# Stores of ScalarE's results: from SyncE's queue to ScalarE's own

## The chip, the cores and the metric

The kernel runs on one core of one Trainium2 chip. The core has five engines, each with its own stream of instructions that it works through in order: TensorE (PE: matmuls, and PEld, the loads of its weights), VectorE (DVE), ScalarE (ACT), GpSimd (POOL) and SyncE (SP), which here only issues transfers (DMAs). They wait for each other through semaphores. Transfers between the chip's main memory and the core's own memory are issued by an engine and carried out by 16 DMA engines. The metric is the device time of one execution in microseconds (us).

## The reference, cut to what matters

Two blocks over a sequence of 2048 positions of width 1024, in float32. The first normalizes, projects, and runs a diagonal state-space scan (S5) over one half of the channels beside a gated short convolution over the other; the second is a modulated layer with a convolution, a bidirectional state-space scan (SSD), a Fourier mix and a gated feed-forward net.

```python
def first_block(x, norm_gain, w_in, ssm_..., w_glu, b_glu, conv_w, w_out, final_norm_gain):
    xn = rmsnorm(h, norm_gain)
    proj = xn @ w_in                       # u_ssm, z_ssm, h_conv, b_conv, c_conv, z_conv
    y_ssm = s5_mixer(u_ssm, ...) * silu(z_ssm)      # scan, gelu, then a gate by w_glu
    y_conv = short_conv_mixer(h_conv, b_conv, c_conv, conv_w) * silu(z_conv)
    h = h + concat(y_ssm, y_conv) @ w_out
    return rmsnorm(h, final_norm_gain)

def second_block(x, c, ctx, c_ctx, w_ada, ...):
    mx = silu(c) @ w_ada + b_ada           # shifts, scales and gates (modulation)
    hx = modulate(rms_norm(x, g_pre_mix), sm_x, cm_x)
    u_f, z, xs, B, C, dt = mixer_inputs(hx, w_in, conv_w, ...)
    y = ssd_bidir(xs, B, C, dt, ...)
    x = x + gm_x * rms_norm(mixer_output(u_f, z, xs, y, ...), g_post_mix)
    x = x + gf_x * rms_norm(swiglu(modulate(...), w_gate, w_up, w_down), g_post_ffn)
```

## The kernel before

The sequence is cut into four blocks of 512 positions (b = 0 to 3). All products are made by `mtile`: a weight tile of 128 x 1024 is loaded (`wraw`, three buffers, L110), ACT casts it to its upper part (`whi`, two buffers, L112), DVE or POOL makes the rest (`wlo`, L115), and PE runs 24 matmuls of 512 columns: 16 with `whi` (L126, L127) and 8 with `wlo` (L130). So for each weight tile PE needs one cast of ACT.

Stages, as they lie in the profile's time: parameters of the scan and the first projection of blocks 0 and 1 (`a1_units`, `s5_params`; 0 to 350 us); the projection of blocks 2 and 3, woven with the scan (`s5_units`), the modulation (`mod_units`) and the first block's gate and output (`a2_units`; 350 to 830 us); the rest of these with the context (830 to 1090 us); stage B, the second block's projection and convolution (`b_units`; 1090 to 1650 us); then scan, mix and feed-forward net.

`s5_units` runs two halves of the sequence (tb) with eight channel groups (cg) each. `enter` loads Ug, s5G (one buffer) and a table, makes two banks of products (L660, L662: eight matmuls each), and DVE scans them (L666 to L683); `leave` loads s5C (one buffer) and s5M, makes the output with 12 matmuls (L704 to L706), and ACT puts it through a gelu into Yg (L707). After every second group Yg, which has 128 partitions, is stored to Yd in main memory by 16 transfers of 16 x 8 x 64 elements (L712). There are eight such bursts in the program, 128 transfers. `mod_units` is a chain of 48 steps: each multiplies the two halves of a weight tile that the step before it has loaded (L940, `mraw`, two buffers in all) and then issues the two loads for the next (L951).

The other stores of the change: Ud, Gd and ZSd before 830 us, and in stage B UFd, XTd, XSd, BTd, CTd, SBd and a part of Z2d, each one transfer behind the ACT instruction that makes its result.

The program is written in Python against a tile framework: a scheduler with priorities (`high_priority` raises those of the weights' loads and casts) puts the instructions of each engine in order, and hands each transfer one of eight completion counters in turn, whichever engine issues it. A transfer waits until the one before it on its counter, that is the transfer eight earlier, has landed. In the kernel before, SP issues all 2037 transfers in one queue.

Of the kernel before, what the change touches and what calls it, by code (L numbers as in the profile page):

```python
# [17 lines left out]
P = 128  # L18
# [43 lines left out]
class Kernel:  # L62
# [335 lines left out]
    def s5_params(self, pp):  # L398
# [124 lines left out]
        def matrices(bt):  # L523
# [56 lines left out]
            nc.scalar.mul(Gt[:, :, P + 64:256], pv[:, :, 0], -1.0)  # L580
            nc.sync.dma_start(out=self.Gd[bt], in_=Gt)
            pk = self.bank("ss")
# [53 lines left out]
    def s5_units(self, tb, sp):  # L636
# [49 lines left out]
        def leave(cg):  # L686
# [21 lines left out]
            if q == 1:  # L708
                c0 = qt * 128
                for t in range(T8):  # L710
                    for i in range(2):
                        nc.sync.dma_start(  # L712
                            out=self.Yd[2 * tb + i, c0:c0 + 128, t, :].rearrange("(g h) k -> h g k", h=GH),
                            in_=Yg[t * GH:(t + 1) * GH, :, i * 64:(i + 1) * 64])
# [62 lines left out]
    def a1_units(self, b, ops):  # L777
# [13 lines left out]
        def u(j):  # L791
# [6 lines left out]
            else:  # L798
                nc.scalar.copy(uk, kt(ps))
            nc.sync.dma_start(out=self.Ud[tb, j * P:(j + 1) * P, :, hf * 64:(hf + 1) * 64],  # L800
                              in_=us.rearrange("p (t k) -> p t k", t=T8))
# [40 lines left out]
        def zs(j):  # L842
            ps = mt(4 + j)
            t = self.tmp("zs")
            silu(t, ps)
            nc.sync.dma_start(out=self.ZSd[b, :, j], in_=t)

# [293 lines left out]
    def uf_dt(self, x, c, X, b):  # L1141
# [11 lines left out]
        if b is not None:  # L1153
            u = self.tmp("uf", (P, FW))
            nc.scalar.copy(u, ps[:, 0:FW])
            nc.sync.dma_start(out=self.UFd[4 * b + c], in_=u)

# [68 lines left out]
    def b_units(self, b, ops, bp):  # L1226
# [22 lines left out]
        def conv(m):  # L1249
# [7 lines left out]
            def turn():  # L1257
                if m < 6:
                    self.transposes(s, TB, st["xs"][:, :, m * P:(m + 1) * P])
                    if m == 5:  # L1260
                        nc.sync.dma_start(out=self.XTd[b], in_=st["xs"])
                elif m < 10:
# [4 lines left out]
            if m < 6:  # L1267
                nc.sync.dma_start(out=self.XSd[b, :, m], in_=s)
            elif m < 10:
                nc.sync.dma_start(out=self.BTd[b, :, m - 6], in_=s)  # L1270
            else:
                nc.sync.dma_start(out=self.CTd[b, :, m - 10], in_=s)

        def gate(m):
# [7 lines left out]
            else:  # L1282
                nc.scalar.activation(z, ps, AF.Silu)
            nc.sync.dma_start(out=self.Z2d[b, :, m], in_=z)

# [3 lines left out]
        def state(c):  # L1289
# [7 lines left out]
            for g, ps in self.states(st["xw"], st["B"], c):  # L1297
# [3 lines left out]
                nc.scalar.copy(sb[:, hs], ps[:, 192:384].rearrange("p (r e) -> p r e", r=HG))  # L1301
            nc.sync.dma_start(out=self.SBd[4 * b + c].rearrange("p (h e) -> p h e", e=64), in_=sb)
            if c < 3:
# [654 lines left out]
```

## Time and profile before

| | |
|---|---|
| median of 3 runs | 3636.63 us (3629.4 to 3638.18) |
| profiled execution | 3634.7 us, of which the span of the core is 3632.8 us |
| PE busy | 3462.0 us (95%) |
| DVE, ACT, POOL busy | 2147.9, 1461.9, 965.3 us |
| granted clock of PE, mean | 0.98 |

The span is the time from the first to the last instruction. Busy is the time in which an engine has an instruction at work; waiting, and issuing a transfer, are not counted. The granted clock is that of PE, as a share of full speed. The views behind the prediction are shown as rows further down.

### The profile page before, as it was taken

The page shows a single profiled execution, that of the slowest core. Times are in us where ns is not written, and L with a number is a line of the kernel's source. Part 1 is how long each engine was busy: PE and PEld are TensorE (multiplying, and loading weights), DVE is VectorE, ACT ScalarE, POOL GpSimd, SP SyncE. Part 2 cuts the span into 40 slices and gives each one's busy share as a digit, 9 for nine tenths or more (in the row PEclk, how much of TensorE's full clock was granted, in tenths as well). Part 3 has the DMA queues.
Part 4 walks back from the last instruction along what each step waited for, and adds up shares of the span by engine and source line. Part 5 has one row for each costly group of instructions (what it writes and reads, how often), then busy time and mean ns, then how long its engine had stood idle before and what let it go on. Part 6 is the DMA issues. An engine that isn't in the chain of part 4 may idle for free.

```text
span 3632.8 us, 46986 instructions
## 1 busy us (share of the span) xinstructions
PE 3462.0 (95%) x16602; PEld 2831.0 (78%) x16602; DVE 2147.9 (59%) x3991; ACT 1461.9 (40%) x2350; POOL 965.3 (27%) x931
## 2 busy tenths in 40 slices
PE   8899999988989999999999999999999999999998
PEld 6677888776778888876777788877888778887887
DVE  8765534446687577777756544566445664454334
ACT  3233232234444344335535533355333553343222
POOL 1764233232353453343213101131011220110001
PEclk9999999999989999999999999999999999999999
DMA  6467565677654565466554334443345443444232
GB/s 199 156 190 223 191 210 175 203 230 241 211 191 153 178 204 172 163 205 203 164 186 137 118 111 155 155 149 120 111 135 171 140 130 111 127 153 130 83 113 76
DMA packets 322508, 588.14 MB, mean 162 GB/s; under 512 B 73952, under 2 KB 150624, under 8 KB 321376
## 3 DMA queue, kind: packets, MB, share of 16 engines
q1 hardware_dynamic: 322272, 585.13, 51.1%
q8 instruction: 132, 2.16, 0.2%
q14 instruction: 104, 0.85, 0.1%
HBM read 472.63 MB, written 112.36 MB: 161 GB/s over the span
## 4 chain that ended last, share of the span: by engine, by line
PE 60%; DVE 6%; DMA 4%; ACT 2%; issue 1%; POOL 1%; SPq 0%; POOLq 0%; DVEq 0%; ACTq 0%
PE mm L130 17%; PE mm L126 17%; PE mm L127 17%; PE ss L1125 1%; PE nb L940 1%; PE ss L1473 1%; PE ss L1523 1%; DVE cy L1038 1%; DMA outT<-n_t 1%; PE nb L1501 1%; PE ss L1138 1%; PE mm L1149 1%; PE mm L1150 0%; PE mm L1151 0%; PE nb L192 0%
## 5 line engine op out<-in xcount | busy, mean ns | idle before, releaser
L112 ACT CAST whi<-wraw 128x1024 fp32r<-128x1024 f32 (+3 forms) x634 | 568.9, 898 | 1044.3 <-PE mm L127 758.0
L115 DVE TENSOR_TENSOR wlo<-wraw,whi 128x1024 fp32r<-128x1024 f32 (+3 forms) x516 | 538.2, 1044 | 698.2 <-PE mm L130 487.3
L126 PE MATMUL mm<-xh,whi 128*128 128x512 f32 (+1 forms) x2000 | 801.2, 403 | 49.4 <-ACT whi L112 30.1
L127 PE MATMUL mm<-xl,whi 128*128 128x512 f32 (+1 forms) x2000 | 787.8, 396 | 5.8 <-DVE xl L142 3.6
L152 POOL TENSOR_TENSOR n_acc<-n_acc,n_sq 128x512 f32<-128x512 f32 (+1 forms) x175 | 229.5, 1315 | 1365.5 <-ACT n_sq L151 1337.9
L126 PE MATMUL mm<-dxh,whi 128*128 128x512 f32 x1408 | 549.9, 391 | 1.7 <-ACT dxh L997 1.7
L127 PE MATMUL mm<-dxl,whi 128*128 128x512 f32 x1408 | 548.6, 390 | 1.6 <-DVE dxl L998 1.5
L130 PE MATMUL mm<-xh,wlo 128*128 128x512 f32 (+1 forms) x2000 | 500.2, 392 | 9.9 <-DVE wlo L115 9.6
L126 PEld LDWEIGHTS mm<-xh,whi 128*128 128x128 f32 x2000 | 385.7, 193 | 138.7 <-ACT whi L112 40.9
L127 PEld LDWEIGHTS mm<-xl,whi 128*128 128x128 f32 x2000 | 385.7, 193 | 86.1 <-DVE xl L142 6.6
L130 PEld LDWEIGHTS mm<-xh,wlo 128*128 128x128 f32 x2000 | 375.7, 191 | 89.9 <-DVE wlo L115 12.9
L115 POOL TENSOR_TENSOR wlo<-wraw,whi 128x1024 fp32r<-128x1024 f32 (+1 forms) x118 | 284.1, 2410 | 549.0 <-ACT whi L112 268.0
L130 PE MATMUL mm<-dxh,wlo 128*128 128x512 f32 x1408 | 349.7, 389 | 0.0
L126 PEld LDWEIGHTS mm<-dxh,whi 128*128 128x128 f32 x1408 | 264.1, 188 | 57.7 <-ACT dxh L997 3.0
L127 PEld LDWEIGHTS mm<-dxl,whi 128*128 128x128 f32 x1408 | 264.3, 188 | 57.2 <-DVE dxl L998 2.8
L130 PEld LDWEIGHTS mm<-dxh,wlo 128*128 128x128 f32 x1408 | 263.6, 188 | 54.3
L126 PE MATMUL mm<-hh,whi 128*128 128x512 f32 (+1 forms) x744 | 285.5, 390 | 5.0 <-ACT hh L141 4.7
L1038 DVE SCALAR_TENSOR_TENSOR cy<-mm,vecs,cy 128x504 f32<-128x504 f32 (+5 forms) x396 | 266.9, 690 | 27.6 <-ACT cy L1032 24.4
L127 PE MATMUL mm<-hl,whi 128*128 128x512 f32 (+1 forms) x744 | 280.5, 382 | 2.0 <-DVE hl L142 2.0
L130 PE MATMUL mm<-hh,wlo 128*128 128x512 f32 (+1 forms) x744 | 199.3, 383 | 0.0
L126 PEld LDWEIGHTS mm<-hh,whi 128*128 128x128 f32 x744 | 139.7, 189 | 36.7 <-ACT hh L141 9.4
L127 PEld LDWEIGHTS mm<-hl,whi 128*128 128x128 f32 x744 | 140.5, 189 | 30.4 <-DVE hl L142 5.2
(473 smaller groups left out, 4510.7 us busy)
## 6 DMA issues: line engine op xcount, KB each, us to landing
wraw<-w_in SPq DMA_DIRECT2D x186, 512.0 KB, 4.5
wraw<-w_gate SPq DMA_DIRECT2D x88, 512.0 KB, 3.7
wraw<-w_up SPq DMA_DIRECT2D x88, 512.0 KB, 3.6
wraw<-w_out SPq DMA_DIRECT2D x64, 512.0 KB, 3.9
mraw<-w_ada SPq DMA_DIRECT2D x96, 256.0 KB, 3.7
n_x<-xT SPq DMA_DIRECT2D x85, 256.0 KB, 4.7
n_x<-X1d SPq DMA_DIRECT2D x80, 256.0 KB, 4.0
n_x<-X2d SPq DMA_DIRECT2D x72, 256.0 KB, 4.0
```

Source lines behind the costliest of these rows:

```text
L112: nc.scalar.copy(hi, raw)
L115: eng.tensor_tensor(lo, raw, hi.bitcast(F32), ALU.subtract)
L126: nc.tensor.matmul(ps, lhsT=hi[:, s], rhs=xh, start=k == ks[0], stop=False)
L127: nc.tensor.matmul(ps, lhsT=hi[:, s], rhs=xl, start=False, stop=False)
L130: nc.tensor.matmul(ps, lhsT=lo[:, s], rhs=rhs(k)[0], start=False, stop=k == ks[-1])
L152: nc.gpsimd.tensor_tensor(acc, acc, sq, ALU.add)
L940: nc.tensor.matmul(ps, lhsT=raws[k // 4][:, k % 4 * P:(k % 4 + 1) * P], rhs=sc[:, k, 0:n], start=k == 0, stop=k == KD - 1)
L1038: nc.vector.scalar_tensor_tensor(yr[:, :, lo:hi], pr[:, :, lo + d:hi + d], w(k), yr[:, :, lo:hi], ALU.mult, ALU.add)
L1125: nc.tensor.matmul(ps, lhsT=B_tm[:, c, g], rhs=xw[:, g].rearrange("p d r e -> p (d r e)"), start=True, stop=True)
L1138: nc.tensor.transpose(ps[:, c], src[:, c * P:(c + 1) * P], self.ident)
L1149: nc.tensor.matmul(ps, lhsT=ah, rhs=wh[:, s], start=(k == 0), stop=False)
L1473: nc.tensor.matmul(ps, lhsT=CT[:, g, c * P:(c + 1) * P], rhs=hFB[:, g].rearrange("p d e -> p (d e)"), start=True, stop=True)
```

## The change

At ten places `nc.sync.dma_start` becomes `nc.scalar.dma_start`: the stores of results that ACT makes are issued by ACT itself, all other transfers by SP as before. Where ACT makes the result in some blocks only (Ud for b > 0, Z2d for b = 0), so does the choice of queue. It is 262 transfers of 2037: Yd 128, Ud 12, ZSd 16, Gd 8, UFd 16, XTd 4, XSd 24, BTd 16, CTd 16, Z2d 6, SBd 16.

```diff
@@ matrices of the scan
-            nc.sync.dma_start(out=self.Gd[bt], in_=Gt)
+            nc.scalar.dma_start(out=self.Gd[bt], in_=Gt)
@@ s5_units, leave
-                        nc.sync.dma_start(
+                        nc.scalar.dma_start(
                             out=self.Yd[2 * tb + i, c0:c0 + 128, t, :].rearrange("(g h) k -> h g k", h=GH),
                             in_=Yg[t * GH:(t + 1) * GH, :, i * 64:(i + 1) * 64])
@@ a1_units, u and zs
-            nc.sync.dma_start(out=self.Ud[tb, j * P:(j + 1) * P, :, hf * 64:(hf + 1) * 64],
+            (nc.scalar if b else nc.sync).dma_start(out=self.Ud[tb, j * P:(j + 1) * P, :, hf * 64:(hf + 1) * 64],
                               in_=us.rearrange("p (t k) -> p t k", t=T8))
-            nc.sync.dma_start(out=self.ZSd[b, :, j], in_=t)
+            nc.scalar.dma_start(out=self.ZSd[b, :, j], in_=t)
@@ stage B
-            nc.sync.dma_start(out=self.UFd[4 * b + c], in_=u)
+            nc.scalar.dma_start(out=self.UFd[4 * b + c], in_=u)
-                        nc.sync.dma_start(out=self.XTd[b], in_=st["xs"])
+                        nc.scalar.dma_start(out=self.XTd[b], in_=st["xs"])
-                nc.sync.dma_start(out=self.XSd[b, :, m], in_=s)
+                nc.scalar.dma_start(out=self.XSd[b, :, m], in_=s)
-                nc.sync.dma_start(out=self.BTd[b, :, m - 6], in_=s)
+                nc.scalar.dma_start(out=self.BTd[b, :, m - 6], in_=s)
-                nc.sync.dma_start(out=self.CTd[b, :, m - 10], in_=s)
+                nc.scalar.dma_start(out=self.CTd[b, :, m - 10], in_=s)
-            nc.sync.dma_start(out=self.Z2d[b, :, m], in_=z)
+            (nc.sync if b else nc.scalar).dma_start(out=self.Z2d[b, :, m], in_=z)
-            nc.sync.dma_start(out=self.SBd[4 * b + c].rearrange("p (h e) -> p h e", e=64), in_=sb)
+            nc.scalar.dma_start(out=self.SBd[4 * b + c].rearrange("p (h e) -> p h e", e=64), in_=sb)
```

The scheduler orders the program anew with it: all engines' orders differ in the first 1700 us or so, and ACT has four more loads of its function tables.

First place, the fourth burst of Yd (Yg_4382). ACT before: the casts whi follow Yg directly.

```order
L707 ACT_TABLE_LOAD
L707 ACTIVATE Yg_4382<-ss_4775 128x512
L141 CAST xh_4130<-n_t_4805 128x512
L112 CAST whi_4881<-wraw_4879 128x1024
L799 COPY us_4842<-mm_4817 128x64x8
L112 CAST whi_4915<-wraw_4913 128x1024
L799 COPY us_4876<-mm_4851 128x64x8
L112 CAST whi_4949<-wraw_4947 128x1024
```

ACT now:

```order
L707 ACT_TABLE_LOAD
L707 ACTIVATE Yg_4382<-ss_4775 128x512
L712 DMA Yd<-Yg_4382 16x8x64
L112 CAST whi_4881<-wraw_4879 128x1024
L712 DMA Yd<-Yg_4382 16x8x64 x15
L112 CAST whi_4915<-wraw_4913 128x1024
L799 COPY us_4842<-mm_4817 128x64x8
L112 CAST whi_4949<-wraw_4947 128x1024
```

The cast whi_4915, which the weight tile mm_4919 needs, moved behind all sixteen stores. On PE a modulation step (L940, a bank nb, two halves of mraw) stood by itself between two weight tiles before; this is the one with the bank nb_5268:

```order
L130 MATMUL mm_5236<-xh_4130,wlo_5234 128x512 x8
L940 MATMUL nb_5268<-sc_104,mraw_5175 128x2 x4
L940 MATMUL nb_5268<-sc_104,mraw_5176 128x2 x4
L126 MATMUL mm_5289<-xh_4130,whi_5285 128x512
L127 MATMUL mm_5289<-xl_4131,whi_5285 128x512
```

PE now, between the weight tile of whi_4881 and that of whi_4915:

```order
L940 MATMUL nb_5055<-sc_104,mraw_4726 128x2 x4
L940 MATMUL nb_5055<-sc_104,mraw_4727 128x2 x4
L940 MATMUL nb_5164<-sc_104,mraw_5066 128x2 x4
L940 MATMUL nb_5164<-sc_104,mraw_5067 128x2 x4
L940 MATMUL nb_5268<-sc_104,mraw_5175 128x2 x4
L940 MATMUL nb_5268<-sc_104,mraw_5176 128x2 x4
L940 MATMUL nb_5352<-sc_104,mraw_5279 128x2 x4
L940 MATMUL nb_5352<-sc_104,mraw_5280 128x2 x4
L940 MATMUL nb_5469<-sc_104,mraw_5363 128x2 x4
L940 MATMUL nb_5469<-sc_104,mraw_5364 128x2 x4
L940 MATMUL nb_5581<-sc_104,mraw_5480 128x2 x4
L126 MATMUL mm_4919<-xh_4130,whi_4915 128x512
```

Five modulation steps and the first half of a sixth moved ahead of mm_4919, one directly behind the other.

Second place, the seventh burst (Yg_5744). ACT before and now:

```order
L151 ACTIVATE n_sq_6369<-us_6366 128x512
L151 ACTIVATE n_sq_6442<-us_6439 128x512
L707 ACTIVATE Yg_5744<-ss_6376 128x512
L112 CAST whi_6515<-wraw_6513 128x1024
L112 CAST whi_6562<-wraw_6560 128x1024
```

```order
L151 ACTIVATE n_sq_6369<-us_6366 128x512
L707 ACTIVATE Yg_5744<-ss_6376 128x512
L712 DMA Yd<-Yg_5744 16x8x64 x16
L112 CAST whi_6515<-wraw_6513 128x1024
L151 ACTIVATE n_sq_6442<-us_6439 128x512
```

Here, too, the next cast stands behind the stores. On PE the second of two output groups of the scan (ss_6705; the first is ss_6601) stood within the weight tile of whi_6741 before, a tile and a half behind the first:

```order
L126 MATMUL mm_6745<-yh_6208,whi_6741 128x512
L127 MATMUL mm_6745<-yl_6209,whi_6741 128x512
L704 MATMUL ss_6705<-Ug_6250,s5M_6703 128x128
L705 MATMUL ss_6705<-s5w_1238_6498,s5C_6701 128x128
L706 MATMUL ss_6705<-s5w_1239_6499,s5C_6701 128x128
```

PE now:

```order
L705 MATMUL ss_6601<-s5w_1198_6274,s5C_6597 128x128
L706 MATMUL ss_6601<-s5w_1199_6275,s5C_6597 128x128
L704 MATMUL ss_6705<-Ug_6250,s5M_6703 128x128
L705 MATMUL ss_6705<-s5w_1238_6498,s5C_6701 128x128
L706 MATMUL ss_6705<-s5w_1239_6499,s5C_6701 128x128
```

It moved directly behind the first group, and both ahead of the tile mm_6519 of whi_6515.

## Rows read from the trace of the kernel before

**Rows 1.** The page: busy time of each engine; the chain's shares by engine.

```profile
PE 3462.0 (95%) x16602; PEld 2831.0 (78%) x16602; DVE 2147.9 (59%) x3991; ACT 1461.9 (40%) x2350; POOL 965.3 (27%) x931
...
PE 60%; DVE 6%; DMA 4%; ACT 2%; issue 1%; POOL 1%; SPq 0%; POOLq 0%; DVEq 0%; ACTq 0%
```

**Rows 2.** Stretches: length, busy PE, PEld, DVE, ACT, POOL; clock, DMA share, GB/s.

```profile
100.00:200.00 100.00, 85.00 (x356) 66.80 (x355) 71.16 (x114) 28.36 (x42) 72.75 (x115) 0.91 0.53 165
...
350.00:400.00 50.00, 46.37 (x271) 40.35 (x270) 26.52 (x52) 13.42 (x14) 15.60 (x7) 1.00 0.68 224
400.00:500.00 100.00, 97.21 (x546) 85.11 (x545) 56.08 (x111) 29.17 (x34) 29.81 (x13) 0.98 0.59 188
500.00:600.00 100.00, 96.43 (x513) 82.82 (x512) 30.29 (x60) 33.30 (x37) 34.06 (x14) 0.98 0.63 193
600.00:700.00 100.00, 93.95 (x522) 81.69 (x521) 45.48 (x71) 21.99 (x25) 27.26 (x11) 0.98 0.59 186
700.00:830.00 130.00, 111.38 (x519) 89.42 (x518) 68.78 (x89) 50.98 (x71) 38.98 (x21) 0.95 0.76 235
...
1090.00:1400.00 310.00, 305.62 (x1631) 255.48 (x1632) 208.10 (x422) 128.56 (x199) 124.90 (x105) 0.99 0.52 174
```

**Rows 3.** Waits of SP's queue, whole span: total us, times, longest.

```profile
SPq L1272 <- ACT zs L1041: 42.4, 15, 4.1
...
SPq L712 <- ACT Yg L707: 22.8, 6, 7.9
```

**Rows 4.** PE's timeline: start, us, line, operation, [idle before, what ended it].

```profile
631.37 0.77 PE L660 MATMUL ss<-Ug,s5G 128*128 128x128 f32 x2 [2.58 <-DMA s5G<-Gd]
...
656.06 0.46 PE L704 MATMUL ss<-Ug,s5M 128*128 128x128 f32 x2 [2.63 <-DMA s5M<-Md]
...
726.47 0.46 PE L704 MATMUL ss<-Ug,s5M 128*128 128x128 f32 x2 [0.60 <-DMA s5M<-Md]
...
779.97 0.50 PE L126 MATMUL mm<-xh,whi 128*128 128x512 f32 x1 [2.38 <-ACT whi L112]
...
798.66 0.46 PE L704 MATMUL ss<-Ug,s5M 128*128 128x128 f32 x2 [1.62 <-DMA s5M<-Md]
```

**Rows 5.** Issue of two lines' stores, ns min/median/max, first and last start.

```profile
L712 SPq DMA_DIRECT2D Yd<-Yg x128: 302/434/1843, 396.0 to 809.5; - x128
...
L1268 SPq DMA_DIRECT2D XSd<-zs x24: 319/327/863, 1118.3 to 1561.6; - x24
```

**Rows 6.** Timeline: SP's first and longest Yd burst, and a cast of ACT.

```profile
396.02 8.65 SPq L712 DMA_DIRECT2D Yd<-Yg  x16
...
624.75 12.03 SPq L712 DMA_DIRECT2D Yd<-Yg  x16
...
396.13 1.05 ACT L112 CAST whi<-wraw 128x1024 fp32r<-128x1024 f32 x1
```

**Rows 7.** Timeline of ACT: casts for two weight tiles that follow each other.

```profile
447.57 1.05 ACT L112 CAST whi<-wraw 128x1024 fp32r<-128x1024 f32 x1 [1.72 <-PE mm L127]
453.01 1.05 ACT L112 CAST whi<-wraw 128x1024 fp32r<-128x1024 f32 x1 [4.38 <-PE mm L127]
```

**Rows 8.** Half a step; s5 group (ns); mraw to landing: 350 to 830 us, whole.

```profile
582.34 0.95 PE L940 MATMUL nb<-sc,mraw 128*128 128x2 f32 x8
...
L660 PE MATMUL ss<-Ug,s5G x128: 271/275/552, 354.4 to 777.1; 128*128 128x128 f32 x128
...
DMA to landing us min/median/max: 2.6/4.5/8.0
...
mraw<-w_ada SPq DMA_DIRECT2D x96, 256.0 KB, 3.7
```

**Rows 9.** Landing of s5C (L698); timeline of DVE, ends of one scan.

```profile
DMA to landing us min/median/max: 3.5/6.2/8.0
...
387.89 0.69 DVE L666 TENSOR_TENSOR s5w<-ss,s5T 128x512 f32<-128x512 f32 x1 [1.37 <-PE ss L660]
...
396.35 0.69 DVE L683 TENSOR_TENSOR s5w<-s5s,s5T 128x512 f32<-128x512 f32 x1
```

## The prediction

> **What bounds the kernel now.** I read the page's busy times and chain first: TensorE (PE) is busy for 3462.0 of 3632.8 us, ScalarE (ACT) for 1461.9, and the chain of waits is 60% PE [rows 1]. So a store costs or gains something only where it makes PE idle. The table of stretches then shows where PE is idle [rows 2]: 15.0 us from 100 to 200 us, and 34.7 us in the five stretches from 350 to 830 us (480.0 less 46.37, 97.21, 96.43, 93.95 and 111.38), the part in which the S5 scan is woven into the first projection. In 1090 to 1400 us, in stage B, from which 98 of the moved stores come, PE is busy for 305.62 of 310. The orders of PE, ACT, DVE, POOL and SyncE (SP) are the same in both kernels from about 1700 us on, so only what stands before that can change.
>
> The SP queue's own waits look like the case for the change: SP stands 42.4 us in front of one store of stage B, L1272, and 22.8 us in front of Yd's [rows 3]. But a queue that waits costs nothing while its loads are early enough. In the list of PE's idle times I looked for loads that came late behind a Yd burst, and found five places, 2.58, 2.63, 0.60, 2.38 and 1.62 us, **9.8 us in all** [rows 4]: s5G or s5M land late, or a cast of weights starts late because its load did.
>
> **The change part by part.**
>
> *SP is relieved.* 262 stores leave it: 128 of Yd at a median of 434 ns and 134 others near the 327 ns of L1268 [rows 5], 55.6 + 43.8 = about 100 us of issue. A Yd burst held SP for 8.65 us in the first case and 12.03 in the longest [rows 6]. What this gives PE is the 9.8 us of rows 4 if all five go. Bounds: 0 if each of those loads is then late for another reason, and half of the 34.7 us, 17, if loads that come earlier also help waits that I can't trace to SP. I take 9.8.
>
> *ACT takes the issues, one by one.* Stage B's stores (L1156, L1268 to L1284, L1302) come singly and cost ACT about 0.33 us each beside casts that PE asks for once per weight tile, every 5.44 us [rows 7]; ACT is 40% busy. PE is at 98.6% there, so the gain is at most the 4.4 us left; what is queued behind a store is a cast that has 5.4 us. I take 0 (-4 to +2). The stores before 350 us (Ud, ZSd, Gd) are single too; SP runs freer there, ACT may stand behind a store whose counter another transfer holds. Neither is in the trace; I take 0, with a third of the 15.0 us idle in 100 to 200 us, 5, to either side.
>
> *The Yd bursts are the cost.* In before, while SP issued the first burst (396.02 to 404.67), ACT went on at once with a cast of weights at 396.13 [rows 6]. In after, sixteen stores stand on ACT between Yg and the next casts. ACT waits with them: each store waits for the landing of the transfer eight earlier on any queue, and some of these are SP's loads. Behind them stand the casts whi, and behind each cast POOL's wlo, the SP load that reuses wraw, and PE's next weight tile. A hold of 8 to 12 us exceeds what one tile of 5.44 us hides; so the order, too, was changed to cover it: other PE work now stands ahead of the tile whose cast is late. That work isn't free of waits. Five bursts have all stores ahead of a cast, three (the third, sixth and eighth) have casts between their stores.
>
> Fourth burst (first pair of orders): ahead of mm_4919 PE now has five and a half modulation steps in a row, one tile before them. mraw has two buffers, and a step reads both halves. So the next step's load is issued only when the half step before it, 0.95 us [rows 8], has read the buffer, and lands later. Per link PE has two halves, 1.9 us, and the period is 0.95 + the landing L: idle is L - 0.95. L is 3.7 us in the median of the kernel [rows 8]; in the stretch from 350 to 830 us it is 2.6 at least and 4.5 in the median, with SP's queue full. Five links: 13.8 us at 3.7, 8.3 at 2.6, 17.8 at 4.5. I take 3.7, since SP has nothing else to issue between these loads. In before a whole weight tile stood between two steps, more than any of these landings, so that nothing was waited for.
>
> Seventh burst (second pair): two groups of output matmuls (L704 to L706) stand back to back ahead of mm_6519, where weight tiles stood between them. s5C has one buffer: the second group's load can't start before the first has been read, and lands 6.2 us later (3.5 to 8.0) [rows 9]. The second group needs the scan's result as well, 9.2 us after L660's last matmul (387.89 to 397.04, rows 9), of which the first group hides about 3: again 6. So 6.2.
>
> Fifth burst: one bare link (2.75), and one with an s5 group between. Such a group has eight matmuls of L660 and eight of L662, sixteen as in a full step, about 1.9 us [rows 8]: 2.75 - 1.9 = 0.85. Sum 3.6 (at 2.6 and 4.5 us: 1.65 and 5.2). First and second burst: one link with an s5 group between, 0.85 each: 1.7 (0 to 3.3). The three interleaved bursts: 0, at most the longest burst less two tiles, 12.03 - 10.9 = 1.1 each, 3.4.
>
> Sum of the bursts: 13.8 + 6.2 + 3.6 + 1.7 + 0 = **25.3** (8.3 + 3.5 + 1.7 = 13.5 to 17.8 + 8.0 + 5.2 + 3.3 + 3.4 = 37.7).
>
> *The clock.* Where PE is idle more, the clock granted is lower: from 700 to 830 us it is 0.95 with 18.6 us idle, so 5% of 130 us, 6.5 us or 0.35 us for each idle us [rows 2]. For 25.3 - 9.8 = 15.5 us more idle that is **+5.4** (-1 to 13).
>
> The sum, on the profiled execution's own time: 3634.7 + 25.3 - 9.8 + 0 + 0 + 5.4 = 3655.6, rounded to **3656**. This execution is 1.9 us under the median of the runs, 3636.63, whose spread is 3629.4 to 3638.18; I leave that out.
>
> **The rivals.**
>
> *SP's queue decides (faster).* With no burst on it, SP issues the s5 and weight loads 8 to 12 us earlier from 396 us on, and loads land at their least, 2.6 us, since less is in flight. Then two thirds of the idle time from 350 to 830 us go, 23 us, and the bursts cost their low end, 13.5: 3634.7 - 23 + 13.5 - 3.3 of clock = 3622. For it: SP's waits in rows 3, and weight casts that wait for loads. Against it: only 9.8 us of idle time lead back to SP. It decides if the modulation loads land in under 2.7 us and the casts keep ahead. The Trainium skill, "Perfetto Trace Analysis", section "DMA Optimizations", advises giving loads to one engine and stores to another. By that rule the sum would have only the gain: 3634.7 - 9.8 - 3.4 = 3621.5. No run shows it yet; of this rival's chance I give it a third.
>
> *Gain and loss cancel (no change).* The bursts cost the low 13.5, and the relief is its upper 17: 3634.7 - 3.5 - 1.2 = 3630; with bursts of 19 and the 9.8 it is 3634.7 + 9.2 + 3.2 = 3647. For it: stage B, with 98 of the 262 stores, is bound by PE alone.
>
> *The stores are not split off at all (much slower).* The eight counters are shared: ACT's stores wait for SP's loads, those for PE, and PE for the casts behind the stores. If such rings close in every burst, a burst costs its length on SP less one tile: with 8.65 us in the first and 12.03 in the longest, at some 9 us, 3.4 each or 27 in eight, on top of the links: 3656 + 27 + a clock share of up to 9 = 3683 to 3692. Of the order I have seen this in part only (a few stores per burst wait for loads that wait for PE). The Trainium skill, "Perfetto Trace Analysis", section "DMA Instruction — HWDGE (DVE, Sync)", says that the generator of descriptors is shared and is locked while one queue uses it. By that rule a store of ACT may stand behind one issue of SP: sixteen times about 0.33 us, 5 us more per burst; of this rival's chance I give it a third. In before one queue issued everything, so its trace can't show it.
>
> **How the numbers follow.** A measurement of this kernel can tell about 0.3% from no change, 11 us: 3625.7 to 3647.5. Chances: forecast, 3648 to 3672, 0.45; much slower 0.17; cancel 0.24; faster 0.14. So faster 0.14, same 0.24, slower 0.62. Range: the worst sum (bursts 37.7, no relief, clock 13, +2 and +5) is 3692, the best (bursts 13.5, relief 17, clock -1, -4 and -5) 3621; the range leaves out most of the faster rival and the end of the much slower one: 3629 to 3687. The forecast's own range is 3645 to 3672.
>
> **What would show it.** In the changed kernel: the five places of rows 4 gone or under 1 us; in front of L940 five idle times of 2 to 3.5 us each in one clump near 540 us, released by mraw's load; in front of L705 one of about 6 us near 770 us, by s5C or s5w; sixteen Yd stores on ACT in 8 to 14 us and a cast right behind; 1090 to 1400 us as busy as before. It is wrong if PE's idle time from 350 to 830 us is below 40 us, if the casts themselves, not the links, end most of it (then the stores' holding of ACT was mis-sized), or if the difference comes before 350 us or in stage B.

## Result, and the profile after the change

The changed kernel takes **3659.81 us** (median of 4 runs, 3652.65 to 3665.2) against 3635.78 for the kernel before, measured beside it (3629.4 to 3638.18): a ratio of 1.0068, 95% interval 1.0046 to 1.009. It is 0.7% slower. The prediction was 3656, and its largest chance stood on slower. The profiled execution has a span of 3658.4 us, 25.6 more than before. One execution among all the runs below, one of after_dve_td, took 13104.05 us at a granted clock of 0.588 and is left out of its ratio.

The page of the kernel after, busy times (answers the first line of [rows 1]):

```profile
PE 3474.8 (95%) x16602; PEld 2848.5 (78%) x16602; DVE 2155.2 (59%) x3991; ACT 1456.4 (40%) x2346; POOL 964.6 (26%) x931
```

The same 16602 matmuls kept PE busy for 12.8 us longer (3474.8 less 3462.0), and the other 12.8 us are idle time. So half of the loss is matmuls that took longer; the granted clocks below say where. ACT has four instructions fewer (x2346 for x2350): the changed order has 71 loads of its function tables for 75, four fewer, and not four more as the section on the change says. Stretches of the kernel after (columns as in [rows 2]); stage B is taken later, at 1115 to 1425 us, since the work arrives there some 30 us later:

```profile
100.00:200.00 100.00, 69.58 (x291) 54.45 (x291) 68.47 (x108) 25.10 (x38) 87.42 (x133) 0.86 0.46 148
350.00:400.00 50.00, 49.60 (x264) 42.40 (x263) 18.41 (x35) 15.12 (x16) 18.90 (x8) 1.00 0.68 197
400.00:500.00 100.00, 91.94 (x529) 82.47 (x528) 61.19 (x130) 24.95 (x31) 22.61 (x9) 0.90 0.69 220
500.00:600.00 100.00, 93.59 (x446) 81.11 (x445) 24.38 (x40) 30.33 (x34) 28.91 (x12) 0.88 0.60 185
600.00:700.00 100.00, 97.45 (x516) 86.17 (x516) 48.00 (x80) 24.32 (x27) 26.31 (x11) 0.91 0.62 196
700.00:830.00 130.00, 119.00 (x570) 99.88 (x569) 52.74 (x60) 42.13 (x55) 52.56 (x25) 0.95 0.60 182
...
1115.00:1425.00 310.00, 304.99 (x1626) 254.46 (x1625) 210.32 (x412) 127.11 (x205) 130.39 (x115) 0.99 0.51 172
```

Three things stand out. PE's idle time from 100 to 200 us has doubled, 30.4 us for 15.0. From 350 to 830 us it has *fallen*, from 34.7 to 28.4 us (480.0 less the five busy times), while the clock from 400 to 700 us is 0.88 to 0.91 where it was 0.98. Stage B is as before.

The kernel after gets to this stretch some 20 us late and leaves it some 36 us late, so nearly the same matmuls lie before 350 us and from 350 to 830 us in the kernel before (first two lines) as before 370 us and from 370 to 866 us in the kernel after (last two):

```profile
0.00:350.00 350.00, 315.83 (x1362) 250.75 (x1363) 252.27 (x611) 116.98 (x169) 176.57 (x240) 0.96 0.62 189
350.00:830.00 480.00, 445.34 (x2364) 379.40 (x2363) 227.14 (x381) 148.85 (x180) 145.71 (x65) 0.98 0.65 205
0.00:370.00 370.00, 316.31 (x1371) 252.21 (x1372) 250.52 (x614) 118.80 (x169) 171.06 (x240) 0.94 0.60 184
370.00:866.00 496.00, 463.52 (x2355) 400.37 (x2354) 225.56 (x379) 144.98 (x177) 143.72 (x64) 0.92 0.64 197
```

The later of the two stretches takes 16.0 us longer. PE is idle for 32.5 us there where it was 34.7, but busy for 18.2 us more, at a mean clock of 0.92 for 0.98 (behind it 5.9 us of busy time come back). On balance its loss is clock, and none of it waiting. The loss before 350 us is of the other kind: PE's busy time is nearly the same, 316.31 us for 315.83, and the rest of the 20 us is waiting.

To see where the time goes I take, in two traces, the moment at which PE starts the same n-th matmul. The table gives by how many us the second kernel is later than the first, when the second stands at the time named in the heading; names are those of the experiments below. Each trace is one execution, and where PE's orders differ (350 to 1680 us) the n-th matmul isn't always the same work, so columns from 625 to 1650 us are good to some us only; the runs' medians decide on totals:

| first, second | 100 | 200 | 350 | 625 | 1000 | 1650 | 3600 us |
|---|---|---|---|---|---|---|---|
| before, after | -1.6 | 11.9 | 19.9 | 34.4 | 31.6 | 34.5 | 26.1 |
| before, yd_only | -3.2 | -2.3 | -4.6 | 15.4 | 6.6 | 12.9 | 17.7 |
| before, early_only | -1.0 | 11.8 | 19.1 | 25.2 | 30.8 | 34.5 | 27.9 |
| before_sq3, after_sq3 | -0.4 | 13.2 | 22.8 | 37.4 | 37.6 | 38.2 | 38.9 |
| before_td, after_td | -1.7 | -0.8 | 6.1 | 16.7 | 11.7 | 7.7 | 6.2 |
| before_dve_td, after_dve_td | -0.8 | -1.9 | -7.3 | 8.2 | 2.9 | 2.7 | 1.1 (3000 us) |

The first row is the answer to the change: about 20 us before 350 us, another 12 to 15 by 1000 us, nothing in stage B. Behind 1700 us, where all orders are alike, it drifts by some 8 us between these two executions; I have no cause for that. It also says how far two single executions can drift apart: yd_only is 17.7 us behind at 3600 us, where its median is 9 us behind, and the pair with sq3 38.9, where the ratios below give 23.

**The early stretch.** PE's order is the same up to there, and yet it has two waits of 15.36 and 9.42 us. Timeline of PE, kernel after:

```profile
174.32 0.80 PE L126 MATMUL mm<-xh,whi 128*128 128x512 f32 x1 [15.36 <-ACT whi L112]
197.52 0.79 PE L126 MATMUL mm<-xh,whi 128*128 128x512 f32 x1 [9.42 <-ACT whi L112]
```

The largest that the kernel before has between 100 and 350 us, by the same view:

```profile
179.12 0.79 PE L126 MATMUL mm<-xh,whi 128*128 128x512 f32 x1 [6.25 <-ACT whi L112]
```

Both are ended by a cast of weights. On ACT (timeline, kernel after) that cast stands behind squares of the norm (n_sq, L151) and behind a store:

```profile
172.70 0.63 ACT L151 ACTIVATE n_sq<-n_x 128x512 f32<-128x512 f32 x1 [6.98 <-POOL n_acc L152]
...
194.87 0.63 ACT L151 ACTIVATE n_sq<-n_x 128x512 f32<-128x512 f32 x1 [10.78 <-POOL n_acc L152]
...
196.42 1.04 ACT L112 CAST whi<-wraw 128x1024 fp32r<-128x1024 f32 x1 [0.40 <-ACT zs L789]
...
230.61 0.54 ACTq L800 DMA_DIRECT2D Ud<-us  x1
231.25 1.04 ACT L112 CAST whi<-wraw 128x1024 fp32r<-128x1024 f32 x1 [11.77 <-DMA Td<-T]
```

The square waits for POOL: n_sq has two buffers, and the sum n_acc (L152) that frees one stands on POOL behind 24 table products (L408 to L413), of which the last starts at 193.22 us (timeline of POOL, kernel after):

```profile
193.58 3.95 POOL L152 TENSOR_TENSOR n_acc<-n_acc,n_sq 128x512 f32<-128x512 f32 x3
```

The last two lines on ACT are another hold: a Ud store that waits for a Td store of SP, and the cast behind it 11.77 us late. The order shows what changed on ACT (- before, + after): squares that stood behind a cast now stand ahead of it.

```
 L151 ACTIVATE n_sq_2014<-n_x_2012 128x512
+L151 ACTIVATE n_sq_2066<-n_x_2064 128x512
 L112 CAST whi_1690<-wraw_1688 128x1024
-L151 ACTIVATE n_sq_2066<-n_x_2064 128x512
...
 L112 CAST whi_1737<-wraw_1735 128x1024
+L151 ACTIVATE n_sq_2259<-n_x_2257 128x512
+L151 ACTIVATE n_sq_2309<-n_x_2307 128x512
...
 L112 CAST whi_1814<-wraw_1812 128x1024
```

And SP's queue changed. With ScalarE's stores gone, the stores of Td (L624), which POOL makes, moved forward in it, ahead of loads of weights and of x. Waits of SP's queue from 0 to 350 us (total, times, longest), first of the kernel after, then of the kernel before:

```profile
SPq L624 <- POOL T L413: 84.3, 7, 18.0
```

```profile
SPq L624 <- POOL T L413: 56.1, 6, 17.2
```

The longest of them on the timelines of the kernel after (SP, ACT, PE): SP issues a load of weights at 244.88 us and then stands in front of a Td store until 263.34. The next load of weights leaves right behind that store; the cast waits for it for 15.57 us, and PE for the cast for 6.42 us.

```profile
263.34 0.33 SPq L624 DMA_DIRECT2D Td<-T  x1
263.76 1.21 SPq L110 DMA_DIRECT2D wraw<-w_in  x2
268.44 1.04 ACT L112 CAST whi<-wraw 128x1024 fp32r<-128x1024 f32 x1 [15.57 <-DMA wraw<-w_in]
269.54 0.79 PE L126 MATMUL mm<-xh,whi 128*128 128x512 f32 x1 [6.42 <-ACT whi L112]
```

So three suspects stand side by side: POOL's sums (15.36 and 9.42 us of PE's idle time), the Ud store on ACT (3.13 us at 232.34 us) and SP behind Td (6.42 us). The experiments had to part them.

**The fourth Yd burst.** PE's timeline of the kernel after has the predicted clump:

```profile
571.38 1.84 PE L940 MATMUL nb<-sc,mraw 128*128 128x2 f32 x16
575.08 3.54 PE L940 MATMUL nb<-sc,mraw 128*128 128x2 f32 x16 [1.86 <-DMA mraw<-w_ada]
579.74 3.55 PE L940 MATMUL nb<-sc,mraw 128*128 128x2 f32 x16 [1.11 <-DMA mraw<-w_ada]
584.40 3.72 PE L940 MATMUL nb<-sc,mraw 128*128 128x2 f32 x16 [1.10 <-DMA mraw<-w_ada]
589.08 3.66 PE L940 MATMUL nb<-sc,mraw 128*128 128x2 f32 x16 [0.96 <-DMA mraw<-w_ada]
594.10 1.84 PE L940 MATMUL nb<-sc,mraw 128*128 128x2 f32 x8 [1.37 <-DMA mraw<-w_ada]
```

The period is 4.66 us (579.74 less 575.08); the prediction had 0.95 + 3.7 = 4.65. But each step takes 3.54 us instead of 1.84, and the waits are 1.0 to 1.9 us. A stretch of 4 us shows why (columns as in [rows 2]):

```profile
576.00:580.00 4.00, 2.89 (x15) 2.83 (x14) 0.23 (x2) 0.00 (x0) 0.00 (x0) 0.50 0.33 99
```

The granted clock is 0.50, the 1.2 GHz level, through both clumps of modulation steps, in the second also where PE is busy throughout (4.00 of 4 us from 684 to 688 us). ACT, meanwhile, was held by the burst for 23.24 us (timeline of ACT):

```profile
558.96 23.24 ACTq L712 DMA_DIRECT2D Yd<-Yg  x15
582.29 1.04 ACT L112 CAST whi<-wraw 128x1024 fp32r<-128x1024 f32 x1 [22.30 <-PE nb L940]
```

That is twice what SP took for its longest burst [rows 6], and the trace names PE's own steps (L940) as what ended the cast's wait behind it: stores that wait for landings, of loads that wait for PE (in the program two of the fifteen wait on the counter of a load of mraw, whose buffer a modulation step must have read). It isn't the longest: the five bursts that stand whole ahead of a cast (first, second, fourth, fifth and seventh) take ACT 21.13, 19.38, 23.24, 26.86 and 16.47 us. The cast behind the fourth still came 12 us before PE's next tile at 595.80. The five places of [rows 4] are gone, and with them nearly all waits of their kinds: for casts of weights, s5M and s5G PE waited 14.6, 4.8 and 2.9 us from 350 to 830 us before, and 0, 1.1 and 0.4 us from 350 to 870 us after. The largest sums there are now 11.4 us for casts xh (L141), for 4.2 before, and 9.5 us for mraw. Waits at the second, fifth and seventh burst stand in their stead (PE's timeline):

```profile
491.33 0.76 PE L704 MATMUL ss<-Ug,s5M 128*128 128x128 f32 x2 [3.34 <-DVE s5w L668]
...
677.41 1.84 PE L940 MATMUL nb<-sc,mraw 128*128 128x2 f32 x8 [1.72 <-DMA mraw<-w_ada]
...
809.90 0.46 PE L705 MATMUL ss<-s5w,s5C 128*128 128x128 f32 x2 [3.42 <-DMA s5C<-Cd]
```

### The profile page after: what moved, and what is told of

The parts are those of the page before. It is cut to its first block, busy times and chain, and to the rows that moved or that the text cites. A ratio compares the mean times of both kernels' runs of the same rounds, so it can differ in the third digit from the quotient of the medians.

```text
span 3658.4 us, 46950 instructions
## 1 busy us (share of the span) xinstructions
PE 3474.8 (95%) x16602; PEld 2848.5 (78%) x16602; DVE 2155.2 (59%) x3991; ACT 1456.4 (40%) x2346; POOL 964.6 (26%) x931
## 4 chain that ended last, share of the span: by engine, by line
PE 61%; DVE 5%; DMA 2%; POOL 2%; ACT 2%; issue 1%; SPq 0%; POOLq 0%; DVEq 0%; ACTq 0%
PE mm L130 18%; PE mm L126 17%; PE mm L127 17%; PE ss L1125 1%; PE nb L940 1%; PE ss L1473 1%; PE ss L1523 1%; DVE cy L1038 1%; PE nb L1501 1%; POOL xw L1117 1%; PE ss L1138 1%; DMA outT<-n_t 1%; ACT E L1504 1%; PE nb L192 0%; DVE E L1510 0%
## 5 line engine op out<-in xcount | busy, mean ns | idle before, releaser
L152 POOL TENSOR_TENSOR n_acc<-n_acc,n_sq 128x512 f32<-128x512 f32 (+1 forms) x175 | 234.4, 1343 | 1378.3 <-ACT n_sq L151 1347.4
L126 PEld LDWEIGHTS mm<-hh,whi 128*128 128x128 f32 x744 | 139.6, 189 | 34.7 <-ACT hh L141 7.5
L127 PEld LDWEIGHTS mm<-hl,whi 128*128 128x128 f32 x744 | 140.3, 189 | 30.8 <-DVE hl L142 5.8
```

The source lines that it names most:

```text
L126: nc.tensor.matmul(ps, lhsT=hi[:, s], rhs=xh, start=k == ks[0], stop=False)
L127: nc.tensor.matmul(ps, lhsT=hi[:, s], rhs=xl, start=False, stop=False)
L152: nc.gpsimd.tensor_tensor(acc, acc, sq, ALU.add)
```

## Experiments

All were timed in several rounds beside the kernel before, whose median was 3636.60 in the first four, 3635.08 in the next four, 3629.38 and 3632.97 in the rest. The last column is (ratio - 1) times 3635 us.

| kernel | us | ratio | 95% interval | against before, us |
|---|---|---|---|---|
| after | 3659.81 | 1.0068 | 1.0046 to 1.009 | +25 |
| yd_only | 3646.08 | 1.0024 | 1.001 to 1.0037 | +9 |
| early_only | 3663.53 | 1.0071 | 1.0058 to 1.0084 | +26 |
| stage_b_only | 3628.05 | 0.9989 | 0.9974 to 1.0003 | -4 |
| after_sq3 | 3649.48 | 1.0031 | 1.0015 to 1.0046 | +11 |
| before_sq3 | 3621.77 | 0.9967 | 0.9953 to 0.998 | -12 |
| after_dve | 3648.61 | 1.0039 | 1.0025 to 1.0053 | +14 |
| after_dve_td | 3601.63 | 0.9911 | 0.9892 to 0.993 | -32 |
| yd_mraw3 | 3643.32 | 1.0023 | 1.0009 to 1.0036 | +8 |
| before_td | 3664.78 | 1.0101 | 1.0087 to 1.0115 | +37 |
| after_td | 3674.18 | 1.0127 | 1.0112 to 1.0141 | +46 |
| before_dve_td | 3601.34 | 0.9919 | 0.9904 to 0.9933 | -29 |
| noyd_dve_td | 3609.37 | 0.9931 | 0.9914 to 0.9948 | -25 |

### One part of the change alone: yd_only, early_only, stage_b_only

Each is the kernel before with some of the diff's lines on `nc.scalar`: L712; L581, L800 (the `(nc.scalar if b else nc.sync)` of the diff) and L846; or the stores of stage B (L1156, L1261, L1268 to L1284, L1302).

```
-                        nc.sync.dma_start(      # yd_only, L712
+                        nc.scalar.dma_start(
...
-            nc.sync.dma_start(out=self.Gd[bt], in_=Gt)      # early_only, one of three
+            nc.scalar.dma_start(out=self.Gd[bt], in_=Gt)
...
-            nc.sync.dma_start(out=self.UFd[4 * b + c], in_=u)   # stage_b_only, one of seven
+            nc.scalar.dma_start(out=self.UFd[4 * b + c], in_=u)
```

> Only the 128 Yd stores (L712) go to ACT, all others stay on SP. The orders of PE and ACT are those of before up to the first burst near 390 us, and have the clumps of modulation steps behind it. Theory A (what the two traces show: PE comes out of the first 300 us about 20 us late, and loses about 12 to 14 more by 830 us): 8 to 16 us slower than before, PE on time at 350 us, idle times in front of L940 of 1 to 2 us each. The prediction as it was made (the bursts are the whole cost, 25.3 less 9.8 and 5.4 of clock): 21 us slower. Rival (the stores before 350 us are the whole cost): within 4 us of before.

> Only the stores of Gd, Ud and ZSd (L581, L800, L846) go to ACT; Yd and stage B's stay on SP. In the first 300 us the orders of PE, ACT and POOL are those of the changed kernel. Theory A: 16 to 22 us slower than before, all of it between 160 and 270 us, with PE idle for about 15 and 9 us in front of casts that stand on ACT behind n_sq, which waits for POOL's n_acc. The prediction as it was made: 0, at most 5 us to either side. Rival (the loss before 300 us comes with the Yd stores or stage B's through the shared counters): within 4 us of before.

> Only stage B's stores (UFd, XTd, XSd, BTd, CTd, Z2d, SBd) go to ACT; before 1090 us everything is as in before. All theories, and the prediction: within 4 us of before, PE as busy there (98 to 99% from 1090 to 1400 us).

Yd alone costs 9 us; it is 4.6 us early at 350 us and 15.4 late at 625, behind the same clump. The early stores alone cost 26 us, as much as the whole change and more than the 16 to 22 expected, and 19.1 us of it by 350 us. Stage B's 98 stores cost nothing that can be told from zero. So the step of the prediction that put the early stores at 0 is wrong, and not the one on stage B.

The parts don't add: early_only is also 12 us later in the table at 1000 us than at 350 (30.8 less 19.1), with no Yd store moved. Its waits there are for s5 loads and for casts, the kind of [rows 4] but longer, in an order of the projection that differs from before's and after's. With Yd moved on top (after), the clump costs PE, those waits go, and at 1000 us after and early_only are within 1 us of each other.

### POOL's sums: after_sq3, before_sq3, after_dve

A third buffer for every third square, in the changed kernel and in the kernel before; then, in the changed kernel, the sums of blocks 1 to 3 on VectorE instead of POOL. PE's order stays.

```
-            sq = self.t(self.np_, (P, acc.shape[1]), "n_sq", bufs=2)
+            sq = self.tmp("n_sq3", bufs=1) if third else self.t(self.np_, (P, acc.shape[1]), "n_sq", bufs=2)
...
-            nc.gpsimd.tensor_tensor(acc, acc, sq, ALU.add)      # after_dve
+            (eng or nc.gpsimd).tensor_tensor(acc, acc, sq, ALU.add)
```

> The changed kernel with a third buffer for n_sq in the preparation of blocks 1 to 3; the orders of all engines stay those of the changed kernel, instruction for instruction. Theory A1 (the loss before 300 us is that the new order puts two or three n_sq ahead of a cast while POOL's n_acc, which frees their two buffers, stands behind a block of tables): the idle times near 174 and 197 us go, 14 to 22 us faster than the changed kernel, 3638 to 3646 us. Rival A2 (the stores themselves hold ACT, through counters that wait for POOL's tables): nothing of that changes, within 4 us of the changed kernel.

> The kernel before with the same third buffer; its orders stay the same, too. One n_sq that waits 10 us stands ahead of a cast there (175.5 us), with 6.25 us of idle PE behind it. Theory A1: 3 to 8 us faster than before. Rival A2: within 2 us of before.

> The changed kernel, with the sums of squares of blocks 1 to 3 (n_acc, L152) added by DVE instead of POOL. PE's order stays, and on ACT only one n_sq stands ahead of each of the first casts. Theory A1 (part of the loss before 300 us is ACT standing at an n_sq whose buffer POOL frees late): 8 to 18 us faster than the changed kernel, 3642 to 3652 us, and the waits of ACT for n_acc (17.8 us) go. What would be left of the loss before 300 us is theory A3: SP stands in front of Td stores that wait for POOL's tables (84.3 us in the changed kernel, 56.1 in before), with loads of weights behind them. Rival A2 (the stores on ACT hold the casts): within 4 us of the changed kernel.

The buffer gives the changed kernel some 13 us (ratio 1.0031 for 1.0068), VectorE's sums some 10. But it gives the kernel before 12 as well (theory A1 had 14 to 22 and 3 to 8): POOL's sums cost both kernels about the same, and between after_sq3 and before_sq3 the difference by the ratios is still 23 us; in the traces 22.8 us are there by 350 us. So the waits for n_acc, which stand so plainly on ACT's timeline, are a real cost and not the change's. What is left in after_sq3 looks like this on PE (timeline), again behind casts:

```profile
167.04 0.79 PE L126 MATMUL mm<-xh,whi 128*128 128x512 f32 x1 [8.37 <-ACT whi L112]
...
183.97 0.79 PE L126 MATMUL mm<-xh,whi 128*128 128x512 f32 x1 [9.82 <-ACT whi L112]
```

and on SP's queue (waits, 0 to 350 us):

```profile
SPq L624 <- POOL T L413: 87.2, 7, 18.0
```

The second of the two waits leads back to that queue (timelines of SP and ACT, after_sq3):

```profile
172.21 0.33 SPq L624 DMA_DIRECT2D Td<-T  x1
...
175.41 0.65 SPq L199 DMA_DIRECT2D n_x<-xT  x1
182.36 0.63 ACT L151 ACTIVATE n_sq<-n_x 128x512 f32<-128x512 f32 x1 [6.35 <-DMA n_x<-xT]
```

SP stands in front of the Td store from 162.95 us on; three loads of x leave behind it, ACT's square waits for one of them, and the cast for PE stands behind the square. Two more waits lead there: 6.37 us at 261.76 us, by late weights as in the kernel after, and 4.67 us at 224.69, by the Ud store that ACT holds until a Td store has landed. These three are 20.9 us; in before_sq3, where SP stands in front of Td for 56.3 us, PE has no wait over 2.6 us from 100 to 350 us. For the 8.37 us at 167.04 the trace gives no such path that before_sq3 wouldn't have, too.

### Td's stores off SP's queue: after_dve_td, before_td, after_td, before_dve_td

The one line that differs, in after_dve, in both kernels bare, and in the kernel before with VectorE's sums:

```
-            nc.sync.dma_start(out=self.Td[bt], in_=st["T"])
+            nc.gpsimd.dma_start(out=self.Td[bt], in_=st["T"])
```

> As the run before, and the eight Td stores (L624), which wait for POOL's tables, are issued by POOL's own queue. Theory A3: SP's waits for POOL's tables (some 84 us) and the idle time near 262 to 270 us in front of a cast whose weights SP loaded late go, another 8 to 15 us faster, close to the kernel before at 300 us. Rival (the tables, not the queue, are late; the loads would come in time anyway): within 3 us of the run before, with the idle time in other places.

> The kernel before with one edit: the Td stores of L624 are issued by POOL's queue instead of SP's. Nothing of ScalarE's stores is moved. Theory Q (in the kernel before, too, SP stands in front of Td stores that wait for POOL, 56 us in front of one, and loads behind them come late): PE's idle time before 350 us falls and the time is 8 to 20 us below before, 3617 to 3628. Rival R (only the changed kernel has that wait in a place that costs PE something; in before the loads behind it are early enough): within 4 us of before, 3632 to 3640. Rival S (POOL, which is the slowest producer of that stretch, loses its own time by issuing the stores, and the squares' sums come later): 3 to 10 us slower, 3639 to 3647.

> The kernel before with the two edits that after_dve_td had over the changed kernel: sums of squares of blocks 1 to 3 on VectorE, Td stores on POOL's queue; ScalarE's stores stay on SP. after_dve_td measured 3601.6 against 3635 of before. Theory U (with Td's stores off SP, the moved ScalarE stores cost only their Yd part, since the loss of the early stretch is gone): this kernel is 5 to 15 us faster than after_dve_td, 3586 to 3597. Rival V (with Td off SP, moving ScalarE's stores as well is what frees SP's loads; the split then pays): this kernel is 10 to 25 us slower than after_dve_td, 3611 to 3627.

> The changed kernel with one edit: the Td stores of L624 are issued by POOL's queue. PE's order is that of the changed kernel. Theory Q (most of the 47 us between after_dve and after_dve_td came from SP's queue, so it comes without the sums on VectorE as well): 25 to 45 us below the changed kernel, 3615 to 3635. Rival W (casts of ScalarE still stand behind squares that wait for POOL's sums, which now also issues Td; only both together free the casts): 0 to 12 us below the changed kernel, 3648 to 3660.

In after_dve the line is worth 47 us (1.0039 to 0.9911), far beyond the 8 to 15 expected, and PE stands almost nowhere from 100 to 200 us:

```profile
100.00:200.00 100.00, 97.43 (x442) 78.73 (x441) 92.16 (x150) 41.30 (x60) 80.91 (x111) 0.98 0.75 227
```

In the bare kernels it costs 37 and 21 us instead (after_td against after, 46 less 25). The order tells why: it moved POOL's sums of this stretch behind the table products of nearly two more blocks (POOL, before_td against before; T_2213, T_2523 are the tables of two blocks), and the cast behind a square waits for all of them.

```
 L409 TENSOR_TENSOR a_437_2215<-Hi_693,Li_691 128x128
-L152 TENSOR_TENSOR n_acc_1847<-n_acc_1847,n_sq_1960 128x512
-L152 TENSOR_TENSOR n_acc_1847<-n_acc_1847,n_sq_2014 128x512
-L152 TENSOR_TENSOR n_acc_1847<-n_acc_1847,n_sq_2066 128x512
 L410 TENSOR_TENSOR T_2213<-a_436_2214,a_437_2215 128x128
...
+L152 TENSOR_TENSOR n_acc_1847<-n_acc_1847,n_sq_1960 128x512
 L410 TENSOR_TENSOR T_2523<-a_499_2524,a_500_2525 128x128
```

PE and ACT in before_td (timelines):

```profile
210.69 0.80 PE L126 MATMUL mm<-xh,whi 128*128 128x512 f32 x1 [59.27 <-ACT whi L112]
...
205.09 0.63 ACT L151 ACTIVATE n_sq<-n_x 128x512 f32<-128x512 f32 x1 [57.10 <-POOL n_acc L152]
```

No theory had foreseen 59 us in one piece: Q missed for both kernels, and so did the rivals; S had the kind (the sums come later) and not the size; and before_dve_td fell between U and V. But set in pairs, the runs answer the question. The change's early loss, by the table at 350 us, is 19.9 us as it stands, 22.8 with the third buffer, 6.1 with Td's stores on POOL's queue, and -7.3 with that and VectorE's sums. Over the whole kernel the change then costs 9 us (46 less 37) or nothing (0.9911 against 0.9919). The bare pair alone would be weak, since a wait of 59 us in both can swallow a difference; the pair without that wait says the same. (Sums on VectorE with Td on SP weren't tried in the kernel before; the third buffer, which takes away the same wait, is the nearest pair.) So the early loss goes with one condition: **the Td stores in SP's queue, which wait for POOL.** Each run's orders of ACT and POOL change with that line, too, so this is what the pairs say and not a single edit. The trace of after_sq3 shows two ways in which these stores cost PE time, 16.2 us of waits by late loads and 4.7 by the Ud store that ACT holds for Td's landing; no run has tested them apart.

### Yd's burst again: yd_mraw3, noyd_dve_td

A third buffer for mraw up to 830 us in yd_only; and after_dve_td with L712 back on SP.

```
-            raws = [self.tmp("mraw", (P, 4 * P)) for _ in range(2)]
+            raws = [self.tmp("mraw", (P, 4 * P), bufs=3 if j < 16 else 2) for _ in range(2)]
...
-                        nc.scalar.dma_start(      # noyd_dve_td, L712
+                        nc.sync.dma_start(
```

> The kernel with only Yd's stores on ACT, and a third buffer for the modulation weights (mraw) up to 830 us. PE's order is that of the kernel with Yd alone up to the second burst; in the fourth burst eight whole steps stand in a row instead of five and a half. Theory B (the steps' cost is the link from a half step's end to the next load's landing, 4.7 us a step, whatever the clock): a period of 3.1 to 3.7 us a step in that row, and 3 to 9 us faster than with Yd alone. Rival B2 (PE at the lower clock is the bound there, 3.5 us a step, and the idle times beside it are small): the same period of 4.7 us, within 2 us of Yd alone.

> after_dve_td with one edit: Yd's stores, L712, go back to SP's queue; the other 134 stores stay on ScalarE's, the sums on VectorE, Td on POOL's queue. Set side by side, after_dve_td is 9 us ahead of before_dve_td by 375 us (the early stores on ScalarE, with nothing that holds it), loses 22 us from there to 600 us (Yd bursts: links and lower clock), and gets 11 back by 900 us. Theory X (the parts add once the early stretch is free of POOL: the early stores gain some 5 to 9 us, Yd's bursts cost 7 to 11): this kernel is at 3588 to 3597, 4 to 13 us under both. Rival Y (the order of the projection that this combination gets loses from 500 to 850 us what the early stretch gains, as the run with the early stores alone did, 18 us there): 3600 to 3615, not under them.

With a third buffer the waits of the clump are gone (yd_mraw3, timeline of PE, and 4 us of it):

```profile
559.94 20.38 PE L940 MATMUL nb<-sc,mraw 128*128 128x2 f32 x96 [0.49 <-DMA mraw<-w_ada]
...
572.00:576.00 4.00, 4.00 (x21) 4.00 (x20) 0.23 (x2) 0.00 (x0) 0.00 (x0) 0.50 0.45 142
```

Six steps in 20.38 us, 3.4 each where yd_only had 4.7. That the links were set by mraw's two buffers is shown. Yet the time changes by less than the measurement tells (1.0023 for 1.0024): each theory was right in one half. PE, now busy throughout, goes on at the clock of 0.50, so a row of steps gains 1.3 us a step and no more; and of these few us nothing is left further on (at 850 us this trace is 1.9 us behind that of yd_only). Where they go, in an order that differs from yd_only's, is open. A step at the full clock takes 1.84 us; at this clock 3.4 is all that can be had.

noyd_dve_td ended on the rival's side: 3609.37, 8 us behind after_dve_td (7 by the ratios; the intervals touch). In the traces, moving Yd back costs 14.3 us at 1000 us, but the execution traced of noyd_dve_td is itself 7 us over its median. So the same 128 stores on ACT cost 9 us in one order of the projection and in another cost nothing, or gain about 7. Why the order that goes with early stores on ACT and Yd on SP (early_only has the same one on PE up to 1120 us) loses some 12 us between 350 and 1000 us is open: its waits are for casts, xh and s5 loads in turn, and none of them was tried alone.

## Why the prediction was right, and where it wasn't

**The total was right, the sum was not.** It had 0 for the early stores, 21 for Yd (25.3 - 9.8 + 5.4) and 0 for stage B; the early stretch has about +20 in the traces, Yd alone +9 in the runs, and stage B 0. That the total came out is luck: the 20 us missing from the early stretch were made up for by Yd's smaller cost, by parts that don't add, and by some 8 us that the traced execution regains behind 1700 us without a known cause.

- **The step that failed: "The stores before 350 us are single too ... I take 0", with 5 us to either side.** It counted the issues of the stores and a possible wait of ACT behind one. It didn't ask what takes their place on SP, which works through its queue in order, too: with them gone Td's stores stood ahead of loads. Measured in place of the 0: 19.9 us by 350 us, and 19.1 with the early stores alone. The prediction did have that ACT may stand behind a store whose counter another transfer holds (11.77 us, once); the larger part, SP behind POOL, it did not have. The rows to look at were there: 56.1 us of waiting in front of L624 in the kernel before, more than the 42.4 us of L1272 [rows 3] and more than for any other line in the first 350 us. The line that a queue waits for most in a stretch is where to ask what a new order puts behind it.
- **Relief: right in kind, too small.** The five places of [rows 4] are gone, but with them 20.8 us of waits for weights, s5M and s5G, not 9.8. That the bursts on SP were their cause isn't shown: three of the five stand 19 to 34 us behind the end of the nearest burst before them, and PE's order changed, too.
- **Links: right in period, wrong in kind.** 4.66 us against 4.65, and about 14.3 us lost in the clump (595.80 - 573.2 = 22.6 less 8.3 of steps at the full clock) against 13.8. But only 6.4 us of it is waiting; the rest is matmuls at half the clock. So two of the prediction's own marks fail: idle time from 350 to 830 us is 28.4 (32.5 over the same work), not 40 or more, and most of the difference comes before 350 us.
- **Clock: mis-sized.** For this stretch the sum had 15.5 us more idle time and 5.4 of clock, 20.9 in all; the trace has 16.0, as 18.2 us of slower matmuls and 2.2 us less idle time. The 5.4 was worked out from idle time, and the kernel after doesn't follow that: from 500 to 600 us it has 6.4 us idle and a clock of 0.88, from 700 to 830 us 11.0 us and 0.95. The clumps of modulation steps ran at 0.50 whether PE waited or not.
- **Fifth and seventh burst:** 1.72 us of waiting in front of a half step at 677.41 us and 0.66 us at 679.91 against 3.6, and 3.42 against 6.2. **The second** has a wait of 3.34 us against 0.85.
- **Yd on ACT:** 16.47 to 26.86 us in the five whole bursts against 8 to 14. The ring of the rival "not split off at all" does close in the fourth, PE's steps ending the hold. That hold cost nothing because the order had put PE work of that length ahead of the cast; the rest of that rival didn't come. Nor did a single store take longer to issue: 365 ns in the median on ACT, 434 on SP [rows 5].
- **Stage B, 0:** right; 304.99 of 310 us busy against 305.62, and stage_b_only within 0.3%.

**On the skill's rule.** In this kernel a split of loads and stores by engine made it 0.68% slower. The Trainium skill, "Perfetto Trace Analysis", section "DMA Optimizations", says that such a split may make sense; the run disagrees here, and what paid, together with the sums on VectorE, was to take from the load queue the stores that wait for the slowest producer. The eight issues of Td took SP about 0.33 us each, 2.6 us in all, and with the sums on VectorE moving them, and the orders of ACT and POOL that came with it, was worth 47. The Trainium skill, "DMA: Bandwidth & Descriptors", section "Issuing engines are not separate DMA queues", says that issuing from several engines only saves the sequencer's issue time; this pair of runs shows a gain eighteen times that: the queue's 87.8 us of waits in front of them went, too, and the other engines' orders changed with the line.

## What to carry to other kernels

Before moving transfers off a queue, list which waits stay on it and what will now stand closer behind them: a store that waits for a slow producer shouldn't stand ahead of a load that PE needs. But look at what the engine that gets it does meanwhile: by itself the move of Td's stores to POOL's queue made both kernels slower, by 37 and 21 us. Where a scheduler rewrites the order, a part of a change is worth what its order makes of it; test parts alone and together, and in both kernels, since a cure that helps the new kernel may help the old one as much. before_dve_td and after_dve_td, 0.8% and 0.9% faster than the kernel before, are the versions to go on from.

## What the runs showed of the hardware

- Rows of modulation steps (matmuls of 128x2) were granted the clock of 0.50 (1.2 GHz) after the first of them, with PE busy for 4.00 of 4 us as well as with waits of 1 to 2 us; the step went from 1.84 to 3.4 or 3.5 us. The first matmuls of the 128x512 tile behind them still took 0.63 us, the later ones 0.39 (kernel after, from 596.37 us).
- Whole bursts of Yd's stores took ScalarE 16.47 to 26.86 us where SP's longest took 12.03 [rows 6], each store waiting for an earlier transfer on its counter; the issue of one took about the same on either.
